# Output product of a two-layer decoder trunk: loads issued in strict order, residual halves and the next layer's loads behind them, late sums held, first splits behind evacuations

## The chip, the cores and the metric

The kernel runs on one core of one Trainium2 chip. The metric is the device time of one execution in microseconds; the time before is the median of three runs. The profiled execution is a further run, taken with the hardware profiler.

## The reference

Two post-norm layers on a sequence of 1024 tokens with width 1024. Layer 0 mixes tokens by differential attention with rotary keys, layer 1 by forgetting attention; each is followed by a gated MLP of width 2816 with a causal width-3 convolution on the gate branch. Cut to what matters here:

```python
def conv_ffn(x, w_in, conv_w, conv_b, w_out):
    gate, up = jnp.split(x @ w_in, 2, axis=-1)
    gate = lax.conv_general_dilated(gate, conv_w[:, None, :], ...) + conv_b
    return (jax.nn.silu(gate) * up) @ w_out

for i in range(DEPTH):                      # DEPTH = 2
    y = diff_attention(h, ...) if i == 0 else forgetting_attention(h, ...)
    h = layer_norm(alpha * h + y, ln1_g[i], ln1_b[i])
    f = conv_ffn(h, ffn_w_in[i], ffn_conv_w[i], ffn_conv_b[i], ffn_w_out[i])
    h = layer_norm(alpha * h + f, ln2_g[i], ln2_b[i])
```

The change lies in the last product, `@ w_out`, of both layers, and at the border to the stage before it.

## The kernel before

**Arithmetic.** All products are in split float32: an operand is copied by ScalarE into a rounded high part (L90) and VectorE subtracts it to get the low part (L92); three matmuls, high x high, high x low and low x high (L101 to L103), make one product of tiles. The function that does this is `split`, so a split is one instruction on ScalarE and one on VectorE.

**The MLP.** Both MLP products run as Strassen-like schemes: a 2 x 2 block product by seven block products m = 1 to 7 in place of eight. The up stage goes over 22 feature tiles f of 128 features; for each it makes the seven products in the order 1, 5, 6, 3, 7, 2, 4, four times 3 matmuls each. Some products accumulate in the PSUM bank of an earlier one (6, 7 and 4 on that of 1, 3 on that of 5), so the bank must have been read (evacuated) before: `take` does it, with a ScalarE copy (L1114) or a VectorE addition (L1116). When the last product of a tile is through, `gated` convolves, applies silu, multiplies, stores the gated tile to DRAM (`ad[f]`, L1156) and forms block sums of it in DRAM (`sd`): for f < 11 by plain stores, for f >= 11 by accumulating DMAs issued by GpSimd (POOL, L1163). The sums of the last two tiles, f = 20 and 21 (`last`), are kept as functions in `late_adds` and run at a step of the output product.

**The output product.** `down_steps` makes 64 steps in four passes over k = 0 to 10 (pairs of feature tiles): products (1, 2), (6, 5), (7, 3) and (4). A step is 4 x 3 matmuls for one product and one k; the last two k of a pass (the last eight of pass four) go as one group. Per k a pass loads strips of 128 x 512: `load_a` the activations (`ha`, L1210, from `ad` or `sd`), `load_b` the weights (`wb`, L1217, from `in_wd`); one weight block is loaded in pairs in other buffers (`wst` or `pt`). The strips lie in the 32 buffers that hold the operands of the up products 1, 5, 3 and 7 until these are through; later a strip is free when it has been split. `weights` makes differences of weight strips in place on VectorE (L1226, L1230). `make` splits both operands into one of six pairs of buffers. At the end of a product, `drain` (L1293) takes each bank into the accumulators `acc`; products 6, 7 and 4 (and 3) then go on in the bank just drained. The accumulators hold the residual, loaded from `hs` in halves by `half` (L1338).

**What sets the order.** The Python code traces the instructions in a step order: `when(i, ...)` puts loads, halves, norm and late sums at step i of the output product (step 0 is its first; negative steps lie in the up stage), and `Ffn.run` makes up to six operand pairs ahead. The framework then fixes at build time, with a model of its own of the durations, in which order each engine and each DMA queue takes its instructions; it may deviate from the traced order where data dependences allow it. At run time each queue is in that order, and semaphores hold an instruction until its operands and buffers are ready. All plain loads and stores are issued by SyncE (SP). `with self.tc.issue_after(ins)` ties the instructions in its block that run on the engine of `ins` behind `ins` in that engine's order, without a wait.

Of the kernel before, what the change touches and what calls it, by code (L numbers as in the profile page):

```python
# [3 lines left out]

# [10 lines left out]
ALU = mybir.AluOpType  # L15
# [30 lines left out]
PSF, PSN, PN17 = (0,), 3, 0  # L46
PN1, PN2, PN3 = 256, 0, 256
PF = (0, 0, 0, 0)
S2, S3 = 1, 0
M7, G4 = 15, 8  # L50
ORDER = (0, 2, 1, 3)
# [6 lines left out]
class Trunk:  # L58
# [1000 lines left out]
    def up_steps(self, l, acc):  # L1059

        nc = self.nc
        self.flip = False
        st, early = {}, []
        seq = [(0, 1), (1, 1), (0, 2), (1, 2), (2, 1), (2, 2)]
        seq += [(f, m) for m in (5, 6, 3, 7, 4) for f in (0, 1)]
        seq += [(2, 5), (2, 6), (2, 3), (2, 7), (3, 1), (2, 4)]
        seq += [(f, m) for f in range(3, NF) for m in (1, 5, 6, 3, 7, 2, 4) if (f, m) != (3, 1)]
        onto = {6: 1, 7: 1, 4: 1, 3: 5}

        def make(f, m):  # L1070
            d = st.setdefault(f, {})
            if m == 1:
                d["wg"] = self.tmp(pool=self.tt, tag="pt") if f == 2 else \
                    self.wp.tile([P, 1024], F32, tag="wst", name=self.nm("wg"), bufs=2)
                nc.sync.dma_start(d["wg"], self.i["wi"][l, f])
            elif m == 5:
                d["wu"] = self.tmp()
                nc.sync.dma_start(d["wu"], self.i["wi"][l, NF + f])
            d[m, "w"] = self.up_operand(d["wg"], d.get("wu"), m)


        def product(f, m):
            d = st[f]
            hl = d.pop((m, "w"))
            more = m in onto
            if more:
                d[m] = d[onto[m]]
            elif f < 3 and (m == 1 or (f, m) == (2, 2)):
                if f != 1 and m == 1:
                    early.append(self.sbank())  # L1090
                n = f == 1 or m == 2
                d[m] = early[-1][:, n * 512:n * 512 + 512]
            else:
                d[m] = self.mbank()
            for i in range(4):
                w = slice(i * P, i * P + P)
                self.mm3(d[m], hl[:, w], hl[:, 512 + i * P:512 + i * P + P], *self.x[m, i],
                         i == 0 and not more, i == 3, more)
                self.pulse()

        def take(f, m):


            d = st[f]
            ps = d[m]
            lo, hi = slice(0, 512), slice(512, 1024)
            if m == 1:
                d["g"] = self.qp.tile([P, 1024], F32, tag=f"q{1 - self.own}", name=self.nm("sg")) \
                    if f < 2 else self.tmp(pool=self.pp, tag="p")
            elif m == 5:  # L1110
                d["b"] = self.tmp(pool=self.tt, tag="pt")
            dst = d["b" if m in (5, 7, 4) else "g"][:, lo if m in (1, 2, 5, 7) else hi]
            if m in (1, 5, 6, 4):
                nc.scalar.copy(dst, ps)  # L1114
            else:
                nc.vector.tensor_tensor(dst, ps, dst, op=ALU.add)  # L1116

        def takes(f, m):
            if f == 2 and m in (1, 2):
                return  # L1120
            take(f, m)
            if (f, m) == (1, 4):
                take(2, 1)
            elif (f, m) == (2, 5):
                take(2, 2)
            if m == 4 and f > 1:
                self.gated(l, f, st.pop(f))
            elif f == 2 and m in (6, 3):
                self.gated(l, m == 3, st.pop(m == 3))

        return [([partial(make, *x)], partial(product, *x), partial(takes, *x)) for x in seq]
# [4 lines left out]
    def gated(self, l, f, d):  # L1136

        nc = self.nc
        cw, cb = self.cw[l], self.cb[l]
        g = d["g"]  # L1140
        t = self.tmp()
        nc.scalar.activation(t, g, AF.Identity, scale=cw[:, f, 2:3], bias=cb[:, f:f + 1])
        nc.vector.scalar_tensor_tensor(t[:, 1:], g[:, :1023], cw[:, f, 1:2], t[:, 1:],
                                       op0=ALU.mult, op1=ALU.add)
        nc.vector.scalar_tensor_tensor(t[:, 2:], g[:, :1022], cw[:, f, 0:1], t[:, 2:],
                                       op0=ALU.mult, op1=ALU.add)
        nc.scalar.activation(t, t, AF.Silu)
        if f == NF - 1:

            with self.tc.tile_critical():  # L1150
                nc.scalar.preload_act_table_set("natural_log_exp_and_others")
                nc.scalar.copy(t[:, :1], t[:, :1])
        k = f % (NF // 2)
        nc.vector.scalar_tensor_tensor(t[:, :512], t[:, :512], -1.0, d["b"][:, 512:], op0=ALU.mult, op1=ALU.mult)
        nc.vector.tensor_tensor(t[:, 512:], t[:, 512:], d["b"][:, :512], op=ALU.mult)
        nc.sync.dma_start(self.ad[f], t)  # L1156
        last = f > NF - 3
        e = (self.tmp() if last else g)[:, :512]
        nc.vector.tensor_tensor(e, t[:, :512], t[:, 512:], op=ALU.add)

        def adds():
            for out, x in ((self.ad[k][:, 512:], t[:, 512:]), (self.sd["6"][k], t[:, 512:]), (self.sd["3"][k], e)):
                nc.gpsimd.dma_start(out, x, accum_op=ALU.add)  # L1163

        if f == k:
            for r in ("6", "7", "3"):
                nc.sync.dma_start(self.sd[r][k], e)
        elif last:
            self.late_adds.append(adds)
        else:  # L1170
            adds()
# [9 lines left out]
    def down_steps(self, l):  # L1181
        nc = self.nc
        H = NF // 2
        a, b, acc = {}, {}, []
        self.norm2, self.late_adds = None, []
        outs = {1: (0, 0), 2: (0, 0), 6: (0, 1), 5: (1, 1), 7: (1, 1), 3: (0, 1), 4: (1, 0)}
        onto = {6: 1, 7: 1, 4: 1, 3: 5}
        passes = ((1, 2), (6, 5), (7, 3), (4,))
# [12 lines left out]
        def strip(name, dt=F32):  # L1201
# [2 lines left out]
            n_h += 1  # L1204
            return self.xp.tile([P, 512], dt, tag=("xl", "xh")[n_h % 2], name=self.nm(name))

        def load_a(m, k):

            a[m, k] = strip("ha")
            nc.sync.dma_start(a[m, k], self.sd[str(m)][k] if m in (3, 6, 7) else  # L1210
                              self.ad[k + (0 if m in (1, 5) else H)][:, lo if m < 3 else hi])

        def load_b(n, k):

            def load(t, r):
                b[r, k] = t
                nc.sync.dma_start(t, w[(r // 10 - 1) * H + k][:, lo if r % 10 == 1 else hi])  # L1217

            if n < 0 and k % 2 == 0:
                self.pair = self.wp.tile([P, 1024], F32, tag="wst", name=self.nm("wb"), bufs=2) if k % 4 else \  # L1220
                    self.tmp(pool=self.tt, tag="pt")
            for r in ((11,), (12, 22), (22, 12), (21,), (21,))[n]:
                load(self.pair[:, k % 2 * 512:k % 2 * 512 + 512] if n < 0 else strip("wb"), r)

        def sub(dst, x, y):
            nc.vector.tensor_tensor(dst, x, y, op=ALU.subtract)  # L1226
# [22 lines left out]
        def make(m, k):  # L1249
            nonlocal n_a  # L1250
            if m == 4 and k >= H - 3:
                at, bt = [[strip("oa", F32R) for _ in range(2)] for _ in range(2)]
            else:
                self.flip = not self.flip
                bt = self.wp.tile([P, 1024], F32R, tag="wh" if self.flip else "wl", name=self.nm("wo"))
                j = n_a % 6
                n_a += 1
                at = self.qtile(1 - self.own) if j == 0 else \
                    self.tp.tile([P, 1024], F32R, tag="of", name=self.nm("oa"), bufs=1) if j == 1 else \
                    self.pp.tile([P, 1024], F32R, tag="p", name=self.nm("oa"))  # L1260
                at, bt = [[t[:, lo], t[:, hi]] for t in (at, bt)]
            ops[m, k] = at, bt
            for t, src in zip((at, bt), (a.pop((m, k)), weights(m, k))):
                self.split(*t, src)

        banks = {}

# [67 lines left out]

        def half(tt, c):
            cs = slice(c * 512, c * 512 + 512)
            nc.sync.dma_start(acc[tt][:, cs], self.hs[tt][:, cs])  # L1338


        for tt in range(8):
            when(4, load_acc, tt)
            when(11 + tt if tt < 4 else 20 + tt, half, tt, int(tt > 3))
            when((30 if tt < 4 else 44) + tt, half, tt, int(tt < 4))

        def norm():
# [1 line left out]

        when(6, norm)
        for j in range(2):  # L1350
            when(9 + 3 * j, lambda j=j: self.late_adds[j]())
        m6 = len(steps) - (H + 1 - G4)
        when(m6 + S2, lambda: self.norm2.root(st[0]))
        for tt in range(4):
# [5 lines left out]
    def run(self):  # L1360
# [4 lines left out]
        self.resid = self.i["x"].rearrange("(t p) d -> t p d", p=P)  # L1365
        for l in range(2):
            self.own = (NP + l) % 2
            self.attention(l)
            self.ff.run()
            self.resid = self.hd  # L1370

# [246 lines left out]
```

## Time and profile before

| | |
|---|---|
| runs | 2447.15, 2448.49, 2451.36 us; median 2448.49 us |
| profiled execution | 2453.07 us, of it span 2451.3 us |
| mean granted clock of TensorE | 0.996 |
| TensorE busy | 2404.3 us of the span, 98% |
| VectorE, ScalarE, GpSimd busy | 1869.8, 1245.4, 198.8 us |
| moved by DMA | 312.20 MB, mean 127 GB/s |
| output product | from about 985 us to 1198 us in layer 0, from about 2225 us to the end in layer 1 |

In the listings, PE is TensorE, DVE VectorE, ACT ScalarE and POOL GpSimd; an engine's name with a q is its queue. A row of a list of waits has who waited, for whom, the total in us, how many times, and the longest. A row of a timeline has the start in us, the duration in us, engine, line, operation, output <- inputs by the program's names and, in square brackets, how long the engine stood idle before it and what ended that. A row of stretches has the stretch, its length, each engine's busy time with the number of its instructions in parentheses, then TensorE's granted clock as a share of full speed, the mean busy share of the 16 DMA engines and the GB/s that they moved.

### The profile page before, as it was taken

To read this page: it belongs to the slowest core of one execution; us is meant where nothing else is said; L and a number is where in the kernel's file an instruction comes from. 1 tells how busy PE (TensorE), PEld (TensorE's weight loads), DVE (VectorE), ACT (ScalarE), POOL (GpSimd) and SP (SyncE) were. 2 spreads that over 40 slices of the span, in tenths; PEclk is the share of its full clock that TensorE was granted. 3 is DMA by queue.
4 is the path that set the end of the run, shared out by engine and by line. 5 is a ranking of instruction groups with operands and counts; after the bars stand their busy time and mean duration, and the time that the engine had idled before them with its cause. 6 is when DMAs were issued, how large, how long until landed. Compare 5 with 4: busy or idle time off the path is not lost. (4 is left out here: it accounts for less than half of the span.)

```text
span 2451.3 us, 33031 instructions
## 1 busy us (share of the span) xinstructions
PE 2404.3 (98%) x11361; PEld 1982.9 (81%) x11361; DVE 1869.8 (76%) x3543; ACT 1245.4 (51%) x2342; POOL 198.8 (8%) x390
## 2 busy tenths in 40 slices
PE   9999999999999999999999999999999999999998
PEld 7888887777888887878778888888878888887787
DVE  5888888989777776667767777778898777776668
ACT  4656666556444444434445555555465444444344
POOL 2111111010000111000100000000010001110000
PEclk9999999999999999999999999999999999999999
DMA  6223324522433556965322222234223345559662
GB/s 184 66 78 96 93 78 122 169 86 78 168 116 133 130 125 172 308 196 175 110 74 67 67 68 67 67 101 141 92 91 133 121 141 123 118 129 308 216 203 84
DMA packets 140456, 312.20 MB, mean 127 GB/s; under 512 B 20816, under 2 KB 27984, under 8 KB 140288
## 3 DMA queue, kind: packets, MB, share of 16 engines
q1 hardware_dynamic: 129824, 291.67, 37.6%
q0 software_dynamic: 10176, 18.36, 4.6%
q8 instruction: 89, 1.46, 0.3%
q14 instruction: 79, 0.65, 0.1%
q10 hardware_dynamic: 288, 0.07, 0.0%
HBM read 194.21 MB, written 82.25 MB: 113 GB/s over the span
## 5 line engine op out<-in xcount | busy, mean ns | idle before, releaser
L101 PE MATMUL m<-xh,wh 128*128 128x512 f32 x768 | 314.2, 409 | 0.3 <-ACT xh L90 0.3
L102 PE MATMUL m<-xl,wh 128*128 128x512 f32 x768 | 301.7, 393 | 1.6 <-DVE xl L92 1.6
L103 PE MATMUL m<-xh,wl 128*128 128x512 f32 x768 | 303.1, 395 | 0.0
L101 PE MATMUL m<-xh,wo 128*128 128x512 f32 x656 | 255.5, 389 | 1.7 <-ACT pt L1114 1.7
L103 PE MATMUL m<-xh,wo 128*128 128x512 f32 x656 | 255.3, 389 | 0.0
L102 PE MATMUL m<-xl,wo 128*128 128x512 f32 x656 | 255.2, 389 | 0.0
L90 ACT ACTIVATE wo<-wg 128x512 fp32r<-128x512 f32 x168 | 106.0, 633 | 226.6 <-PE m L103 215.5
L543 DVE CUSTOM_DVE_ANT_0 s<-s,mask 128x384 f32<-128x384 f32 (+7 forms) x256 | 194.2, 759 | 31.9 <-PE s L537 30.9
L90 ACT ACTIVATE pt<-m 128x512 fp32r<-128x512 f32 (+3 forms) x285 | 131.3, 491 | 115.2 <-PE m L1401 111.2
L101 PE MATMUL m<-q,wo 128*128 128x512 f32 x472 | 184.8, 392 | 3.6 <-DVE pt L1116 3.6
L102 PE MATMUL m<-q,wo 128*128 128x512 f32 x472 | 184.3, 390 | 0.0
L103 PE MATMUL m<-q,wo 128*128 128x512 f32 x472 | 184.2, 390 | 0.0
L92 DVE TENSOR_TENSOR pt<-m,pt 128x512 fp32r<-128x512 f32 (+3 forms) x285 | 151.8, 557 | 39.7 <-ACT pt L90 37.9
L103 PEld LDWEIGHTS m<-xh,wl 128*128 128x128 f32 x768 | 144.7, 188 | 31.1
L101 PEld LDWEIGHTS m<-xh,wh 128*128 128x128 f32 x768 | 145.1, 189 | 26.7 <-DVE pt L92 1.9
L102 PEld LDWEIGHTS m<-xl,wh 128*128 128x128 f32 x768 | 145.3, 189 | 25.5 <-DVE xl L92 1.9
L528 POOL CAST qz<-q 64x128 fp32r<-64x128 f32 x256 | 97.9, 383 | 823.0 <-PE s L537 755.1
L90 ACT ACTIVATE wo<-t 128x512 fp32r<-128x512 f32 x132 | 82.7, 627 | 145.5 <-PE m L103 130.1
L101 PEld LDWEIGHTS m<-xh,wo 128*128 128x128 f32 x656 | 123.1, 188 | 27.9 <-ACT pt L1114 2.6
L103 PEld LDWEIGHTS m<-xh,wo 128*128 128x128 f32 x656 | 123.1, 188 | 26.0 <-DVE wo L92 0.4
L102 PEld LDWEIGHTS m<-xl,wo 128*128 128x128 f32 x656 | 123.2, 188 | 25.6
L536 PE MATMUL s<-q,q 128*128 128x512 f32 (+4 forms) x384 | 132.4, 347 | 2.1 <-ACT wst L581 1.3
(354 smaller groups left out, 5904.3 us busy)
## 6 DMA issues: line engine op xcount, KB each, us to landing
wb<-in_wd SPq DMA_DIRECT2D x142, 256.0 KB, 4.9
wst<-in_w SPq DMA_DIRECT2D x46, 512.0 KB, 3.7
t<-in_wi SPq DMA_DIRECT2D x44, 512.0 KB, 4.6
ad<-t SPq DMA_DIRECT2D x44, 512.0 KB, 3.2
ha<-ad SPq DMA_DIRECT2D x88, 256.0 KB, 7.8
wg<-in_wi SPq DMA_DIRECT2D x42, 512.0 KB, 3.6
ha<-sd SPq DMA_DIRECT2D x66, 256.0 KB, 2.8
q<-q SPq DMA_DIRECT2D x128, 128.0 KB, 2.2
```

The lines of the kernel that those rows point to most:

```text
L90: nc.scalar.activation(hi, src, AF.Copy, scale=1.0 if scale is None else scale)
L92: nc.vector.tensor_tensor(lo, src, hi.bitcast(F32), op=ALU.subtract)
L101: mm(out, wh, xh, start=start, stop=False)
L102: mm(out, wh, xl, start=False, stop=False)
L103: mm(out, wl, xh, start=False, stop=stop)
L528: nc.gpsimd.tensor_copy(qz[r:r + 64, :], q[r:r + 64, qt * P:qt * P + P])
L536: nc.tensor.matmul(sb[:, ks], q[:, qt * P:qt * P + P], kd[:, ks], start=True, stop=False)
L543: self.nc.vector.tensor_tensor_reduce(sb[:, :ln], sb[:, :ln], self.mask[:, 1024 - ln:], 1.0, BIG, ALU.add, ALU.min, mn)
```

## The change

- Loads of the output product (`load_a`, `load_b`) go through a new `load`, which ties each load on SP's queue behind the one traced before it (`self.ld` is the last).
- `half` is tied behind the last load traced; the second group of halves (four tiles, c = 1) moves from steps 24 to 27 to steps 35 to 38 (`R2` 31 for 20). `R1` is 11, as the number before.
- The whole SP traffic of layer 1's attention is tied behind layer 0's last load.
- The store of `ad[f]` for f = 20 and 21 is issued by POOL in place of SP.
- The three accumulating sums of each of these two tiles are placed at steps 14 and 18 in place of 9 and 12, and wait until the load traced last before them has landed.
- `take` records the last evacuation on ScalarE and on VectorE; in `make` the splits and the weight differences are tied behind them on their engines.

`EARLY_D` is defined and not used. No arithmetic is changed.

```diff
+EARLY_D, R1, R2, ADDS = 8, 11, 31, (14, 18)
...
-                nc.scalar.copy(dst, ps)
+                self.taken["a"] = nc.scalar.copy(dst, ps).ins
             else:
-                nc.vector.tensor_tensor(dst, ps, dst, op=ALU.add)
+                self.taken["v"] = nc.vector.tensor_tensor(dst, ps, dst, op=ALU.add).ins
...
-        nc.sync.dma_start(self.ad[f], t)
         last = f > NF - 3
+        (nc.gpsimd if last else nc.sync).dma_start(self.ad[f], t)
...
-                nc.gpsimd.dma_start(out, x, accum_op=ALU.add)
+                add = nc.gpsimd.dma_start(out, x, accum_op=ALU.add)
+                if last:
+                    self.tc.add_manual_dep(add.ins, self.ld.ins.name, mybir.DependencyInfo(
+                        mybir.DependencyClass.Sync, mybir.DependencyReason.DATA), reason="late sums")
...
+        def load(dst, src):
+            with self.tc.issue_after(self.ld.ins) if self.ld is not None else nullcontext():
+                self.ld = nc.sync.dma_start(dst, src)
+
         def load_a(m, k):
...
-            nc.sync.dma_start(a[m, k], self.sd[str(m)][k] if m in (3, 6, 7) else
-                              self.ad[k + (0 if m in (1, 5) else H)][:, lo if m < 3 else hi])
+            load(a[m, k], self.sd[str(m)][k] if m in (3, 6, 7) else
+                 self.ad[k + (0 if m in (1, 5) else H)][:, lo if m < 3 else hi])
...
-            for t, src in zip((at, bt), (a.pop((m, k)), weights(m, k))):
-                self.split(*t, src)
+            with self.tc.issue_after(self.taken["a"]), self.tc.issue_after(self.taken["v"]):
+                for t, src in zip((at, bt), (a.pop((m, k)), weights(m, k))):
+                    self.split(*t, src)
...
-            nc.sync.dma_start(acc[tt][:, cs], self.hs[tt][:, cs])
+            with self.tc.issue_after(self.ld.ins):
+                nc.sync.dma_start(acc[tt][:, cs], self.hs[tt][:, cs])
...
-            when(11 + tt if tt < 4 else 20 + tt, half, tt, int(tt > 3))
+            when(R1 + tt if tt < 4 else R2 + tt, half, tt, int(tt > 3))
...
-            when(9 + 3 * j, lambda j=j: self.late_adds[j]())
+            when(ADDS[j], lambda j=j: self.late_adds[j]())
...
-            self.attention(l)
+            with self.tc.issue_after(self.ld.ins) if l else nullcontext():
+                self.attention(l)
```

More of the change, by code (lines that the diff above doesn't have):

```diff
@@ L1 @@
 import math
-from contextlib import ExitStack
+from contextlib import ExitStack, nullcontext
 from functools import partial
@@ L1062, in up_steps @@
         self.flip = False
-        st, early = {}, []
+        st, early, self.taken = {}, [], {}
         seq = [(0, 1), (1, 1), (0, 2), (1, 2), (2, 1), (2, 2)]
@@ L1184, in down_steps @@
         a, b, acc = {}, {}, []
-        self.norm2, self.late_adds = None, []
+        self.norm2, self.late_adds, self.ld = None, [], None
         outs = {1: (0, 0), 2: (0, 0), 6: (0, 1), 5: (1, 1), 7: (1, 1), 3: (0, 1), 4: (1, 0)}
@@ L1205, in strip, with fetch @@
             return self.xp.tile([P, 512], dt, tag=("xl", "xh")[n_h % 2], name=self.nm(name))
+        def load(dst, src):
+            with self.tc.issue_after(self.ld.ins) if self.ld is not None else nullcontext():
+                self.ld = nc.sync.dma_start(dst, src)
         def load_a(m, k):
             a[m, k] = strip("ha")
-            nc.sync.dma_start(a[m, k], self.sd[str(m)][k] if m in (3, 6, 7) else
-                              self.ad[k + (0 if m in (1, 5) else H)][:, lo if m < 3 else hi])
+            load(a[m, k], self.sd[str(m)][k] if m in (3, 6, 7) else
+                 self.ad[k + (0 if m in (1, 5) else H)][:, lo if m < 3 else hi])
         def load_b(n, k):
-            def load(t, r):
+            def fetch(t, r):
                 b[r, k] = t
-                nc.sync.dma_start(t, w[(r // 10 - 1) * H + k][:, lo if r % 10 == 1 else hi])
+                load(t, w[(r // 10 - 1) * H + k][:, lo if r % 10 == 1 else hi])
             if n < 0 and k % 2 == 0:
@@ L1222, in load_b @@
             for r in ((11,), (12, 22), (22, 12), (21,), (21,))[n]:
-                load(self.pair[:, k % 2 * 512:k % 2 * 512 + 512] if n < 0 else strip("wb"), r)
+                fetch(self.pair[:, k % 2 * 512:k % 2 * 512 + 512] if n < 0 else strip("wb"), r)
         def sub(dst, x, y):
```

## The prediction

> **What bounds the kernel now.** First the page's busy times, then the list of waits of TensorE (PE), summed over the run.
>
> ```profile
> PE 2404.3 (98%) x11361; PEld 1982.9 (81%) x11361; DVE 1869.8 (76%) x3543; ACT 1245.4 (51%) x2342; POOL 198.8 (8%) x390
> ...
> PE s L101 <- DVE acc L1293: 9.2, 4, 3.4
> ...
> PE m L101 <- DVE pt L1116: 3.6, 2, 1.8
> PE m L101 <- ACT pt L1114: 1.7, 2, 1.3
> ```
>
> TensorE is busy for 98% of the span, so only its own gaps can be won. Three waits belong to the stretch that the diff touches: before the first matmul of an output product that reuses a PSUM bank it waits for the drain of that bank (L1293, 9.2 us in four waits), and at the end of the up products for an evacuation (L1116 and L1114, 5.3 us in four). The next view cuts both layers' stretches into slices of 5 us; after the times come TensorE's busy time and, at the end of a row, granted clock, DMA share and GB/s.
>
> ```profile
> 980.00:985.00 5.00, 4.31 (x13) 3.46 (x14) 4.25 (x7) 1.59 (x2) 0.00 (x0) 0.72 1.05 390
> 985.00:990.00 5.00, 5.00 (x22) 4.05 (x22) 3.22 (x5) 4.01 (x7) 0.00 (x0) 0.94 1.00 368
> ...
> 1050.00:1055.00 5.00, 4.20 (x12) 3.37 (x13) 4.93 (x12) 1.95 (x4) 0.00 (x0) 0.66 0.75 256
> ...
> 2220.00:2225.00 5.00, 3.17 (x15) 2.30 (x14) 3.09 (x5) 2.92 (x4) 0.00 (x0) 1.00 1.05 399
> 2225.00:2230.00 5.00, 5.00 (x24) 4.14 (x23) 4.36 (x5) 3.73 (x6) 0.00 (x0) 1.00 1.05 387
> 2230.00:2235.00 5.00, 5.00 (x24) 4.14 (x23) 2.00 (x4) 2.70 (x5) 0.00 (x0) 1.00 0.36 133
> 2235.00:2240.00 5.00, 5.00 (x24) 4.14 (x23) 4.30 (x7) 2.12 (x4) 2.68 (x3) 1.00 0.81 186
> 2240.00:2245.00 5.00, 5.00 (x24) 4.14 (x23) 0.00 (x0) 0.00 (x0) 0.00 (x0) 1.00 1.09 249
> ...
> 2290.00:2295.00 5.00, 3.18 (x8) 2.00 (x7) 5.00 (x12) 2.71 (x5) 0.00 (x0) 0.50 0.35 105
> 2295.00:2300.00 5.00, 5.00 (x21) 4.06 (x20) 5.00 (x10) 2.22 (x4) 0.00 (x0) 0.87 0.66 207
> ```
>
> The gaps cost more than their length: after three of the four places the granted clock falls. While busy, TensorE loses 4.31 x 0.28 + 5.00 x 0.06 = 1.5 us after the evacuation waits of layer 0, 4.20 x 0.34 = 1.4 us after the drain waits of layer 0, and 3.18 x 0.50 + 5.00 x 0.13 = 2.2 us after those of layer 1; at 2220 the clock stays at 1.00. So the evacuations are worth 5.3 + 1.5 = **6.8 us**, the drains 9.2 + 1.4 + 2.2 = **12.8 us**, together 19.6 us (0.8%). That is the most these edits can bring.
>
> Behind the waits stand in-order engines. The timelines of the last layer show it:
>
> ```profile
> 2209.27 0.69 DVE L92 TENSOR_TENSOR q<-ha,q 128x512 fp32r<-128x512 f32 x1
> ...
> 2220.56 0.63 ACT L90 ACTIVATE q<-ha 128x512 fp32r<-128x512 f32 x1 [2.85 <-DMA ha<-ad]
> 2221.22 0.69 DVE L92 TENSOR_TENSOR q<-ha,q 128x512 fp32r<-128x512 f32 x1 [2.11 <-ACT q L90]
> 2221.83 0.68 DVE L1116 TENSOR_TENSOR pt<-m,pt 128x512 f32<-128x512 f32 x1
> 2222.57 0.50 PE L101 MATMUL m<-q,wo 128*128 128x512 f32 x1 [1.82 <-DVE pt L1116]
> ...
> 2286.06 0.69 DVE L1226 TENSOR_TENSOR wb<-wb,wb 128x512 f32<-128x512 f32 x1 [6.80 <-DMA wb<-in_wd]
> ...
> 2287.40 1.28 DVE L1293 SCALAR_TENSOR_TENSOR acc<-acc,s 128x512 f32<-128x512 f32 x2
> 2288.82 0.47 PE L101 MATMUL s<-wo,oa 128*128 128x512 f32 x1 [3.40 <-DVE acc L1293]
> 2292.95 0.80 PE L101 MATMUL s<-wo,oa 128*128 128x512 f32 x1 [1.82 <-DVE acc L1293]
> ...
> 1043.92 0.69 DVE L1226 TENSOR_TENSOR wb<-wb,wb 128x512 f32<-128x512 f32 x1 [7.47 <-DMA wb<-in_wd]
> ```
>
> At 2222 a split of the output product (L92), placed ahead of the evacuation, waits for a load, and the evacuation waits behind it. At 2286 a weight difference for k = 5 of the second pass, needed ten steps (some 25 us) later, holds VectorE for 6.80 us while the drains of the first pass stand behind it. Layer 0 does the same (7.47 us).
>
> **The change, part by part.**
>
> *Splits behind evacuations.* No instruction is added; only order. In trace order one operand pair, (1, 0), precedes the evacuation of product 7 instead of about five. The evacuations then wait for TensorE alone: 6.8 us gone, and I take all of it; the bounds are 0 and 6.8. What is late next: the splits that stood ahead. On VectorE these are, from 2209.27 to 2221.22, ten of about 0.6 us, 6 us that move behind the evacuations. The cover is VectorE's idle time in 2220 to 2235 by the rows above, 1.91 + 0.64 + 3.00 = 5.6 us, and a step of 12 matmuls (24 in a slice of 5 us, so 2.5 us) asks for only two splits there. It is just enough on the whole, but the last gating shares the time, so I charge 1 us per layer, **2 us**; bounds 0 and the whole 6 us per layer.
>
> *Stores of f = 20 and 21 to POOL; late sums held.* SP's own waits, its queue, and POOL's:
>
> ```profile
> SPq L1156 <- ACTq L1150: 5.4, 1, 5.4
> ...
> 2227.32 0.96 SPq L1210 DMA_DIRECT2D ha<-ad  x2
> 2234.99 0.32 SPq L1156 DMA_DIRECT2D ad<-t  x1
> ...
> 2208.77 0.89 POOL L1163 DMA_DIRECT2D ad<-t  x1 [16.38 <-DVE wo L92]
> 2235.37 0.86 POOL L1163 DMA_DIRECT2D ad<-t  x1 [23.92 <-DVE t L1155]
> ...
> 994.91 1.16 POOL L637 MEMSET wf<- 128x128 f32 x1
> 1192.22 0.81 POOL L1537 TENSOR_TENSOR acc<-acc,lg 128x256 f32<-128x256 f32 x1 [196.15 <-ACT acc L1536]
> ```
>
> SP stood from 2228.3 to 2235.0 before the store of f = 21 and moved 133 GB/s instead of 387: 3.3 us of loads at full rate. On POOL the store holds nothing up at once, but load (2, 10) reads it, and in strict order all later loads stand behind that load; only the loads between gain, so I count 3 us of earlier arrival, none of it on TensorE by itself. POOL pays one more issue of about 0.9 us per store. The three sums of each of the two tiles (0.79 MB) move from 2208 and 2235 to behind the landing of a load of the second pass, k = 2 and k = 4. In 2235 to 2245 the loads and sums moved 2.18 MB where 387 GB/s would be 3.87 MB: 4.4 us of load time, estimated for one set and the restart. It is not removed but put 20 to 30 us later, beside the loads for k = 4 to 6. Behind the waiting sums POOL has only the memset of L637 and then nothing until 1192: free. Who reads the sums is load k = 9 and 10 of the second pass, ten steps (about 25 us) behind their issue: no wait. Without that cover all loads behind them would stand for a landing.
>
> *Loads strict, residual halves behind, R2 31 for 20.* The queue ahead of the load that held VectorE:
>
> ```profile
> 2269.34 0.84 SPq L1338 DMA_DIRECT2D acc<-hs  x2
> ...
> 2277.70 1.07 SPq L1338 DMA_DIRECT2D acc<-hs  x2
> 2278.87 0.62 SPq L1217 DMA_DIRECT2D wb<-in_wd  x1
> ...
> 2278.87 7.10 DMA wb<-in_wd
> ```
>
> These are the first and the last of four such pairs: eight residual halves of 256 KB, 2.1 MB or 5.4 us at 387 GB/s, go out ahead of this load though they belong to steps 24 and later. Behind the loads of steps 30 to 51 they no longer compete. With the 3 us above, the k = 5 weights land about 8 us earlier, more than the 6.80 and 7.47 us for which VectorE stood. So the long wait goes. But the second wait at each boundary (1.82 us here) comes from splits placed between the drains, and nothing in the diff orders a split or a weight difference against a drain. Of 12.8 us I take **9.7 us**, leaving about 1.5 us per layer; the bounds are 12.8 us and a loss, below. The moved halves are wanted at the drains of step 38 and later and can be issued some ten steps earlier: free.
>
> *Next layer's loads behind.* Its first slab is loaded early and used late:
>
> ```profile
> 1046.21 0.42 SPq L110 DMA_DIRECT2D wst<-in_w  x1
> 1150.80 0.33 SPq L1217 DMA_DIRECT2D wb<-in_wd  x1
> 1179.61 1.07 ACT L90 ACTIVATE wh<-wst 128x1024 fp32r<-128x1024 f32 x1 [0.45 <-PE s L103]
> ```
>
> From the last load at 1150.80 to the use there are 29 us, enough for loads of a few us: nothing lost. If it came later than that, the gate logits of layer 1 would wait.
>
> **Sum:** 6.8 + 9.7 - 2.0 = 14.5 us. The profiled execution took 2453.07 us, 4.6 us above the median of the runs, 2448.49; it becomes 2438.6, and the median **2434.0 us**.
>
> On the clock, the page "TensorE: Matmul & The Clock Gate" of the Trainium skill, Part 1, says that the half rate follows after an idle window of about 3.4 us. This trace differs: 0.66 and 0.72 follow waits of 2.5 and 1.8 us, while 1.00 follows another of 1.8 us. By the page only the wait of 3.40 us would lose clock, and the most to be won would be 2.9 us smaller than by the rows; the rows decide here.
>
> **The rivals.** (a) *Only the evacuations gain* (chance 0.18). Weight differences for k = 6 or 7 are placed ahead of the drains in place of k = 5, since strict order brings their loads forward, and VectorE stands as before. For: nothing ties them to the drains. Against: 8 us of earlier arrival. 6.8 - 2.0 = 4.8 us, 2443.7 us.
>
> (b) *No change* (0.12): as (a), and the moved splits starve the first steps by as much as the evacuations give, 3.4 us per layer, within the 6 us bound. 2448.5 us. Against it is VectorE's 5.6 us of idle time.
>
> (c) *Slower* (0.12): the held sums fall beside the very loads that VectorE waits for. A stand of 6.80 us gave TensorE 5.2 us of waits and 2.2 us of lost clock. The drains turn to a net loss when they cost 4.8 us more than now, that is 2.4 us per layer or a stand of about 9 us. With a set's whole 4.4 us on top of the 6.80, and as much again for k = 7, a stand of 15.6 us costs 8.8 us more per layer: 17.6 - 4.8 = 12.8 us slower, 2461.3 us. Against: loads then have lost 2.1 MB of halves from their queue. The page "DMA: Bandwidth & Descriptors" of the Trainium skill, Queues, rings and completion order, says that an engine takes packets in turn from the queues that have work, which speaks for this case; in the queues' shares over 2235 to 2245 (packets, MB, share of the DMA engines) the trace agrees:
>
> ```profile
> q1 hardware_dynamic: 638, 1.44, 50.7%
> q0 software_dynamic: 393, 0.74, 44.2%
> ```
>
> The sums' queue took nearly half of the engines for a third of the bytes.
>
> The forecast itself has 0.58. Its own range is 2428 to 2440: all 19.6 us won with the scatter of the runs below, and half of the drains above. The whole range reaches over (a) and (b), to 2450; below 2427 there is nothing to win. About 0.2% (4.9 us) is what a measurement of this kernel tells from no change; since (a) lies at that bound, half of its chance goes to each side: faster 0.67, same 0.21, slower 0.12.
>
> **What would show it.** Right: no wait of TensorE for L1116 or L1114 in the up products; VectorE's idle time before the first L1226 after the first pass under 3 us; DMA rate near 387 in the slice where SP now stands; no residual half between the loads of the first 25 steps; POOL's sums some 20 to 30 us later. Wrong: TensorE waiting for L92 in the first output steps, a longer wait for L1293, or loads standing behind the read of f = 21's store until splits run dry.

## The result, and the profile after

The changed kernel takes 2433.72 us, the median of five runs (2432.52 to 2439.96), where the kernel before takes 2448.49: ratio 0.994, interval 0.9925 to 0.9955, some 14.7 us less. A second series gave 0.9941 (0.9928 to 0.9954); each ratio in this document is taken against the kernel before in the same series. The forecast was 2434.0 us. The execution whose profile is read first is the slowest of its five (2439.96 us, span 2438.2); the second series has a profile of its own, of 2434.04 us, span 2432.3. Of the lines named here, the numbers are one to nine higher than before: evacuations are L1115 and L1117, the drain L1302, the weight differences L1234 and L1238, splits L91 and L93, matmuls L102 to L104, loads L1213.

The list of TensorE's waits after, first profile, the rows of the touched stretch:

```profile
PE s L102 <- DVE acc L1302: 4.0, 2, 2.3
...
PE s L104 <- DVE oa L93: 0.6, 1, 0.6
```

Of the waits at the end of the up products, 5.3 us before, no row is left in this stretch; the drain waits (TensorE waiting for a drain) fell from 9.2 to 4.0 us, all of it in layer 0. In the second profile of the same kernel no drain wait is left at all. The timelines show VectorE's stand, its idle time for the k = 5 weights before the first drain. First profile:

```profile
1038.12 0.69 DVE L1234 TENSOR_TENSOR wb<-wb,wb 128x512 f32<-128x512 f32 x1 [4.98 <-DMA wb<-in_wd]
...
1045.01 0.50 PE L102 MATMUL s<-wo,oa 128*128 128x512 f32 x1 [1.71 <-DVE acc L1302]
...
1100.29 0.69 DVE L1234 TENSOR_TENSOR wb<-wb,wb 128x512 f32<-128x512 f32 x1 [1.86 <-DMA wb<-in_wd]
...
1107.63 0.50 PE L102 MATMUL s<-wo,oa 128*128 128x512 f32 x1 [2.25 <-DVE acc L1302]
...
2272.36 0.69 DVE L1234 TENSOR_TENSOR wb<-wb,wb 128x512 f32<-128x512 f32 x1 [1.35 <-DMA wb<-in_wd]
```

Second profile:

```profile
959.84 1.25 ACT L1143 ACTIVATE t<-p,cb,cw 128x1024 f32<-128x1024 f32 x1
...
1033.96 0.69 DVE L1234 TENSOR_TENSOR wb<-wb,wb 128x512 f32<-128x512 f32 x1 [2.17 <-DMA wb<-in_wd]
...
1098.63 1.87 DVE L1302 SCALAR_TENSOR_TENSOR acc<-acc,m 128x512 f32<-128x512 f32 x3
...
2266.95 0.69 DVE L1234 TENSOR_TENSOR wb<-wb,wb 128x512 f32<-128x512 f32 x1 [2.38 <-DMA wb<-in_wd]
```

The stand was 7.47 and 6.80 us before; it is 4.98 and 1.35 us in the one execution and 2.17 and 2.38 in the other. After the stand of 4.98 us TensorE still waits at the end of pass one, 1.71 us (at 1045.01); after the stands of 1.35 to 2.38 us of this kernel it does not. The other 2.25 us of the 4.0 lie at another place, the end of pass two (1107.63), where TensorE waited for nothing before: there a weight difference of a later pass, at 1100.29, stands ahead of the drains in its turn. At the place that the change was made for, 9.2 us became 1.7.

To compare executions without the scatter of the rest of the kernel, two clocks are used below, both started by the first activation of feature tile f = 20 (L1142 before, L1143 after; 959.84 in the listing above). The *k = 5 clock* is the start of the weight difference that stands right before the first drain of pass one: 1033.96 - 959.84 = 74.1 us. The *pass-two clock* is the start of the group of three drains near the end of pass two: 1098.63 - 959.84 = 138.8 us. Before, in layer 0, they are 1043.92 - 959.01 = 84.9 us (the row of the weight difference is shown in the prediction) and 150.0 us from these rows:

```profile
959.01 1.25 ACT L1142 ACTIVATE t<-p,cb,cw 128x1024 f32<-128x1024 f32 x1
...
1109.00 1.88 DVE L1293 SCALAR_TENSOR_TENSOR acc<-acc,m 128x512 f32<-128x512 f32 x3
```

The table has both clocks (layer 0 / layer 1), worked out from the same rows of each trace, TensorE's waits for evacuations and for drains (us in the touched stretch of both layers, at the ends of all passes), and the measured ratio to the kernel before. A step of 0.001 is 2.4 us. The experiments it names follow.

| kernel | k = 5 clock | evacuations | drains | pass-two clock | ratio (interval) |
|---|---|---|---|---|---|
| before | 84.9 / 84.3 | 5.3 | 9.2 | 150.0 / 149.1 | 1 |
| after, first profile | 77.0 / 73.3 | 0 | 4.0 | 144.0 / 138.3 | 0.994 (0.9925 to 0.9955) |
| after, second series | 74.1 / 74.3 | 0 | 0 | 138.8 / 139.0 | 0.9941 (0.9928 to 0.9954) |
| splits only | 84.8 / 82.2 | 0 | 13.8 | 149.8 / 147.0 | 1.0003 (0.9994 to 1.0012) |
| stores and sums only | 84.5 / 81.4 | 0 | 9.8 | 150.0 / 146.2 | 1.0004 (0.9995 to 1.0013) |
| halves only | 80.7 / 78.6 | 4.4 | 3.0 | 145.6 / 142.1 | 0.9971 (0.996 to 0.9983) |
| order only | 79.2 / 74.7 | 5.5 | 0 | 143.6 / 141.1 | 0.9969 (0.9958 to 0.998) |
| order and splits | 79.4 / 74.4 | 0 | 3.8 | 144.4 / 139.5 | 0.9967 (0.9956 to 0.9979) |
| all but splits | 75.3 / 73.3 | 0.4 | 0.6 | 140.6 / 139.0 | 0.9928 (0.9914 to 0.9941) |
| all but halves | 74.1 / 74.7 | 0 | 1.5 | 141.4 / 138.7 | 0.9952 (0.994 to 0.9965) |
| all but held sums | 75.7 / 75.8 | 0 | 4.7 | 143.6 / 141.3 | 0.9952 (0.9939 to 0.9964) |

Each clock and each wait is one execution; the ratio is the measurement. In the first profile 2.3 us of the drain waits lie at the end of pass two, in "all but held sums" 2.2 us, and in "all but splits" and "all but halves" all of them; in the other rows all lie at the end of pass one.

In the rows without a wait for evacuations to speak of, the k = 5 clock orders the drain waits at the end of pass one. Per layer they are nothing up to 75.3 us, 1.1 to 1.7 us at 75.7 to 77.0, 3.8 us at 79.4, and 4.5 to 8.0 us from 81.4 on. The length of the stand does not: in "order and splits", layer 0, it is 2.29 us, with 3.8 us of drain waits. One row needs care: in layer 0 of "stores and sums only" the clock is no landing of weights (experiment 8).

### The profile page after: what moved, and what is told of

Read it like the earlier page. It is cut to its first block, busy times and chain, and to the rows that moved or that the text cites. A ratio compares the mean times of both kernels' runs of the same rounds, so it can differ in the third digit from the quotient of the medians.

```text
span 2438.2 us, 32989 instructions
## 1 busy us (share of the span) xinstructions
PE 2399.7 (98%) x11361; PEld 1981.7 (81%) x11361; DVE 1866.9 (77%) x3543; ACT 1244.7 (51%) x2342; POOL 200.2 (8%) x394
## 5 line engine op out<-in xcount | busy, mean ns | idle before, releaser
L102 PE MATMUL m<-xh,wh 128*128 128x512 f32 x768 | 314.6, 410 | 1.3 <-ACT xh L91 1.3
L104 PE MATMUL m<-xh,wl 128*128 128x512 f32 x768 | 303.4, 395 | 0.0
L104 PE MATMUL m<-xh,wo 128*128 128x512 f32 x656 | 255.3, 389 | 0.0
L102 PE MATMUL m<-xh,wo 128*128 128x512 f32 x656 | 255.2, 389 | 0.0
L91 ACT ACTIVATE wo<-wg 128x512 fp32r<-128x512 f32 x168 | 106.0, 632 | 226.0 <-PE m L104 215.2
L91 ACT ACTIVATE pt<-m 128x512 fp32r<-128x512 f32 (+3 forms) x285 | 131.3, 491 | 115.2 <-PE m L1412 111.3
L102 PE MATMUL m<-q,wo 128*128 128x512 f32 x472 | 184.1, 390 | 0.0
L104 PE MATMUL m<-q,wo 128*128 128x512 f32 x472 | 183.7, 389 | 0.0
L93 DVE TENSOR_TENSOR pt<-m,pt 128x512 fp32r<-128x512 f32 (+3 forms) x285 | 151.9, 557 | 39.7 <-ACT pt L91 38.1
L104 PEld LDWEIGHTS m<-xh,wl 128*128 128x128 f32 x768 | 145.0, 189 | 31.1
L102 PEld LDWEIGHTS m<-xh,wh 128*128 128x128 f32 x768 | 145.4, 189 | 27.6 <-DVE pt L93 2.1
L103 PEld LDWEIGHTS m<-xl,wh 128*128 128x128 f32 x768 | 145.6, 190 | 25.4 <-DVE xl L93 1.8
L91 ACT ACTIVATE wo<-t 128x512 fp32r<-128x512 f32 x132 | 82.7, 626 | 146.0 <-PE m L104 130.0
L104 PEld LDWEIGHTS m<-xh,wo 128*128 128x128 f32 x656 | 123.2, 188 | 25.8 <-DVE wo L93 0.4
L102 PEld LDWEIGHTS m<-xh,wo 128*128 128x128 f32 x656 | 123.2, 188 | 25.6
```

What stands on the lines that cost most here:

```text
L91: nc.scalar.activation(hi, src, AF.Copy, scale=1.0 if scale is None else scale)
L93: nc.vector.tensor_tensor(lo, src, hi.bitcast(F32), op=ALU.subtract)
L102: mm(out, wh, xh, start=start, stop=False)
L103: mm(out, wh, xl, start=False, stop=False)
L104: mm(out, wl, xh, start=False, stop=stop)
```

## The experiments

**1. The splits alone** (label e1_splits_only), on the kernel before:

```diff
+            with self.tc.issue_after(self.taken["a"]), self.tc.issue_after(self.taken["v"]):
                 for t, src in zip((at, bt), (a.pop((m, k)), weights(m, k))):
                     self.split(*t, src)
```

> The kernel before with one edit: the splits of the output product are placed behind the last evacuations; loads, stores, halves and sums stay as before. Theory (parts add up): the waits of TensorE for the two evacuations (5.3 us) and the lost clock behind them (1.5 us) go, the drain waits stay near 9.2 us: 2448.5 - 6.8 = 2441.7 us. With the 2.0 us that I charged for late splits it would be 2443.7, with waits of TensorE for L93 in the first output steps. Rival (the loads do it all): the evacuations wait as before for something else that stands on VectorE or ScalarE, 2448 us.

Measured: 1.0003 (0.9994 to 1.0012), no gain. The waits and the timeline say where the 5.3 us went:

```profile
PE s L101 <- DVE acc L1294: 13.8, 4, 6.7
...
1043.40 0.69 DVE L1226 TENSOR_TENSOR wb<-wb,wb 128x512 f32<-128x512 f32 x1 [7.63 <-DMA wb<-in_wd]
1046.16 0.77 PE L101 MATMUL s<-wo,oa 128*128 128x512 f32 x1 [6.72 <-DVE acc L1294]
```

No evacuation is waited for any more, and the drains are waited for 13.8 us, where it was 9.2. TensorE comes earlier to the end of pass one and meets the same late weights: the k = 5 clock in layer 0 is 84.8 us for 84.9. The upstream wait had covered part of the downstream one. In layer 1 both clocks are 2.1 us lower than in the profile before; the interval leaves room for a gain of 1.5 us at most, so that part of this is the scatter of single executions. Both theories were wrong, the sum of parts and the rival that let the evacuations wait as before.

**2. All but the splits** (e2_all_but_splits): the changed kernel with the lines above taken back.

> The changed kernel without the order of splits behind evacuations. Theory (parts add up): the evacuation waits come back, 5.3 us and 1.5 us of clock, the drains stay near 4 us: 2433.7 + 6.8 = 2440.5 us. Rival: with the loads in strict order the operand for which the split stood (it waited 2.85 us) lands earlier, so the evacuations hardly wait either, 2434 to 2436 us.

Measured: 0.9928 (0.9914 to 0.9941), the rival's time or better. In its list of waits only this is left of the two places:

```profile
PE s L102 <- DVE acc L1301: 0.6, 1, 0.6
...
PE m L102 <- ACT p L1115: 0.4, 1, 0.4
```

So the evacuations run free without the edit that was made for them, and the whole gain is there. The interval overlaps that of the changed kernel (0.9941, 0.9928 to 0.9954), so taking the edit out is not shown to be faster; that it is needed is refuted.

**3. All but the halves** (e3_halves_free): the halves not tied, and

```diff
-EARLY_D, R1, R2, ADDS = 8, 11, 31, (14, 18)
+EARLY_D, R1, R2, ADDS = 8, 11, 20, (14, 18)
```

> The changed kernel with the residual halves neither tied behind the loads nor moved (R2 20 for 31). Theory (it is the 2.1 MB of halves ahead of the k = 5 weights that made VectorE stand): the stand before the drains grows by about 5.4 us in each layer, drain waits go from 4.0 us back to about 9, 2433.7 + 8.8 = 2442.5 us. Rival (the order of the loads and the store on POOL are enough): stand under 5 us, 2434 to 2436 us.

Measured: 0.9952 (0.994 to 0.9965). The median, 2437.46 us, lies between the two expectations, and the ratio is not separated from the changed kernel. The stand did not come back:

```profile
1036.49 0.69 DVE L1234 TENSOR_TENSOR wb<-wb,wb 128x512 f32<-128x512 f32 x1 [2.18 <-DMA wb<-in_wd]
```

With the loads in strict order the halves no longer delay the k = 5 weights (74.1 and 74.7 us). SyncE's timeline shows where they fit in, in this kernel and then in the second profile of the changed one:

```profile
1019.25 0.91 SPq L1213 DMA_DIRECT2D wb<-in_wd  x2
1020.20 3.04 SPq L1347 DMA_DIRECT2D acc<-hs  x6
1029.92 0.32 SPq L1213 DMA_DIRECT2D ha<-sd  x1
```

```profile
1015.63 0.88 SPq L1213 DMA_DIRECT2D wb<-in_wd  x2
1026.47 0.33 SPq L1213 DMA_DIRECT2D ha<-sd  x1
```

Before the loads for k = 5 SyncE itself stands, in the changed kernel 9.9 us for a split (L93), which is what frees a strip to load into. Six halves go out in this gap; the stand for the split is then 4.8 us.

**4. All but the held sums** (e4_sums_free): the dependence of the sums on a load taken out, `ADDS` (9, 12) for (14, 18).

> The changed kernel with the late sums not held behind loads and called at steps 9 and 12, as before. Theory (a set of sums costs the loads 4.4 us wherever it stands ahead of the k = 5 weights, and one of the two sets stands there in both kernels): the sums are back near 2208 and 2235, the stand before the drains changes by less than 2 us, 2432 to 2436 us. Rival 1 (the held sums beside the k = 5 loads are what leaves 4 us of drain waits in layer 0): these go, 2430 us. Rival 2 (holding them is what frees the loads): the stand grows by 4.4 us per layer, half of it on TensorE with its clock, 2439 us.

Measured: 0.9952 (0.9939 to 0.9964), median 2437.36 us, drain waits 4.7 us. The k = 5 clock is 75.7 and 75.8 us, 1.6 and 1.5 us later than in the second profile of the changed kernel, but between the 77.0 and 73.3 us of the first. That is the first expectation for the weights; the time is 1.4 us above its range. Rival 1 is refuted, since the drain waits did not go; rival 2 asked for a delay of 4.4 us, more than either comparison shows. The ratio is not separated from the changed kernel's, so what holding the sums is worth stays open.

**5. The changed kernel again** (c0_after), no edit.

> The changed kernel once more, as the measure for the other runs of this chip: 2433.7 us, ratio to the kernel before 0.994; drain waits of TensorE near 4 us and no wait for an evacuation of the up products.

Measured: 2434.87 us, 0.9941; its rows stand in the section on the result. The drain waits were expected near 4 us and were none: with one kernel they differ by that much from one execution to the next.

**6. The halves alone** (s1_halves_only), on the kernel before: each half tied behind the last load, R2 31.

> The kernel before with one part alone: the residual halves stand behind the load that was issued last, and the second set of four begins at step 31 for 20. Splits, loads, stores, sums and the next layer as before. Theory A (each part has its own wait): the k = 5 weights land 5.4 us earlier, the drain waits fall from 9.2 to about 2 us with their clock, the evacuation waits stay at 5.3: 2448.5 - 9 = 2439.5 us. Theory B (one late supply; taking the halves back in the changed kernel cost about 3 us only): 3 to 4 us, 2445 us, with several us of drain waits left.

Measured: 0.9971 (0.996 to 0.9983), 7.1 us; between the theories. The weights start 4.2 and 5.7 us earlier, close to the 5.4 us of the halves' bytes, and the drain waits fall by 6.2 us; the evacuation waits stay:

```profile
PE m L102 <- DVE pt L1117: 3.2, 2, 1.6
PE s L102 <- DVE acc L1297: 3.0, 2, 2.0
...
PE m L102 <- ACT pt L1115: 1.2, 1, 1.2
```

**7. The order alone** (s2_order_only), on the kernel before: `load` ties each load behind the one before, nothing else.

> The kernel before with one part alone: every load of the output product is issued behind the one before it. Splits, halves, stores, sums and the next layer as before. Theory A (each part has its own wait): order by itself removes nothing from the queue, so the waits stay, 2446 to 2449 us. Theory B (the operands for the splits that stand ahead of the evacuations, and the k = 5 weights, come late because later loads are issued ahead of them): the evacuation waits go and half of the drain waits, 2437 to 2441 us.

Measured: 0.9969 (0.9958 to 0.998), 7.6 us. Neither theory had it whole: the drains are free altogether, and the evacuations wait as before.

```profile
PE m L102 <- DVE pt L1117: 5.5, 2, 3.3
```

SyncE's timeline shows why. In the prediction's rows the k = 5 weights are issued at 2278.87, the last of several loads and halves, and take 7.10 us to land. With the loads in order they go at 2267.48, although ten halves stand ahead of them in one block, and 3.2 us later the difference has them:

```profile
2257.13 5.87 SPq L1343 DMA_DIRECT2D acc<-hs  x10
...
2267.48 0.81 SPq L1210 DMA_DIRECT2D wb<-in_wd  x2
...
2270.72 0.69 DVE L1231 TENSOR_TENSOR wb<-wb,wb 128x512 f32<-128x512 f32 x1 [0.22 <-DMA wb<-in_wd]
```

From the start of the layer's clock (2201.78 before, 2196.04 here) the issue is at 77.1 and 71.4 us: 5.7 of the 9.6 us by which the weights come earlier in this layer are an earlier issue, the rest a quicker landing.

**8. Stores and sums alone** (s3_stores_and_sums), on the kernel before: the two stores on POOL, the sums held.

> The kernel before with one part alone: the stores of the last two gate tiles on POOL, and their sums held behind loads of the second pass. Splits, loads, halves and the next layer as before. Theory A (each part has its own wait): 3 us of earlier arrival only, 2445 to 2449 us. Theory B (4.4 us of sums and 3 us of standing taken away ahead of the k = 5 weights is what freed the boundary): 7 us earlier landing, drain waits under 3 us, 2440 us.

Measured: 1.0004 (0.9995 to 1.0013), theory A by its time. But the trace repeats experiment 1 by other means: no wait for L1115 or L1117 in the stretch, and

```profile
PE s L102 <- DVE acc L1300: 9.8, 4, 3.5
```

The split that held the evacuation in the prediction's rows stood 2.85 us for its load and started 18.8 us after the start of the layer's clock; here it stands 1.62 us and starts at 14.8 us. So with the first sums and the store out of the way the first strips land sooner. The gain is waited away at the drains. In layer 0, though, VectorE does not stand there for the k = 5 weights but for the split of `wf`, the gate weights of the next layer, and the weight difference then follows without a wait:

```profile
1041.96 0.29 DVE L93 TENSOR_TENSOR wf<-t,wf 128x128 fp32r<-128x128 f32 x1 [6.45 <-ACT wf L91]
```

Stores and sums or the order of splits, each alone, free the evacuations. This fits experiment 2, which needs no order of splits.

**9. Drains first** (d1_drains_first), on the kernel before, no DMA edit:

```diff
+            with self.tc.issue_after(self.drained) if m not in (1, 2) and k > 3 else nullcontext():
                 for t, src in zip((at, bt), (a.pop((m, k)), weights(m, k))):
                     self.split(*t, src)
```

> The kernel before, loads, stores, halves and sums untouched; the weight differences and splits for k = 4 and later of the second to fourth pass are placed behind the last drain of the pass before (VectorE's and ScalarE's order alone). Theory V (the late weights of k = 5 cost time only because the drains stand behind the difference that waits for them; TensorE needs them some 25 us later): the drain waits go from 9.2 us to under 2, the evacuation waits stay near 5, about as with the loads in order alone, 2443 us. Theory S (the loads as such are too late): TensorE waits for the operands of k = 5 in place of the drains, no gain, 2448 us or more.

**10. Drains first, and the splits** (d2_drains_first_splits): that and the edit of experiment 1.

> As the run above, and the first splits of the output product placed behind the evacuations: two changes of order on VectorE and ScalarE, and none of loads, stores, halves or sums. Theory V: both places are free, nothing of the 19.6 us is left to wait for, 2430 to 2435 us, as fast as the changed kernel. Theory S: the time that is won at the evacuations comes back as waits of TensorE for operands of the second pass, as it came back at the drains in the splits alone, 2445 us or more.

Measured: 1.0004 (0.9994 to 1.0013) and 0.9992 (0.9982 to 1.0001), the times of theory S. The waits of the first kernel are those of theory V: 1.6 us for drains and 4.7 us for evacuations. The edit had a side effect, so these times do not decide. It also ties the operands for k = 4 and later of pass four, which TensorE needs at once. In the second kernel, layer 1:

```profile
PE s L102 <- DVE wo L92: 4.3, 1, 4.3
...
2410.00:2415.00 5.00, 5.00 (x24) 4.14 (x23) 5.00 (x11) 1.80 (x7) 0.00 (x0) 1.00 0.00 0
2415.00:2420.00 5.00, 1.66 (x8) 1.04 (x6) 5.00 (x5) 0.49 (x1) 0.00 (x0) 0.93 0.49 200
```

The pass-two clock ends before that place. It is 143.4 and 142.6 us with the first edit alone, for 150.0 and 149.1 before. With both edits it is 144.5 and 138.7 us (layer 0, layer 1), where the splits alone had 149.8 and 147.0 and the changed kernel without a drain wait 138.8 and 139.0:

```profile
959.29 1.25 ACT L1142 ACTIVATE t<-p,cb,cw 128x1024 f32<-128x1024 f32 x1
...
1040.05 0.29 DVE L92 TENSOR_TENSOR wf<-t,wf 128x128 fp32r<-128x128 f32 x1 [2.15 <-ACT wf L90]
...
1103.83 1.88 DVE L1295 SCALAR_TENSOR_TENSOR acc<-acc,m 128x512 f32<-128x512 f32 x3
...
2201.62 1.25 ACT L1142 ACTIVATE t<-p,cb,cw 128x1024 f32<-128x1024 f32 x1
...
2340.34 1.87 DVE L1295 SCALAR_TENSOR_TENSOR acc<-acc,m 128x512 f32<-128x512 f32 x3
```

Up to there theory V holds whole in layer 1, with no load moved, and for half of the gain in layer 0, where TensorE still waited 2.5 us for a drain and 1.6 us for a split. The row at 1040.05 shows what stood ahead of the first drain there: again the split of `wf`, which the new tie leaves out and which layer 1 does not have. One execution of each kernel carries this; a version that ties only passes two and three was not run.

**11. Order and splits** (s5_order_and_splits), on the kernel before, nothing else.

> The kernel before with two parts: the loads in order and the first splits behind the evacuations; halves, stores, sums and the next layer as before. If the two places are worth about 7 us each once the other one is free, and the splits free the one and the order the other: 2434 to 2437 us, all that the changed kernel gains. If the halves and sums ahead of the k = 5 weights still hold the drains once TensorE comes 5 us earlier: 4 to 5 us of drain waits, 2440 us.

Measured: 0.9967 (0.9956 to 0.9979), the second case. The splits add nothing to the order (0.9969) even here: 5.5 us of evacuation waits go and 3.8 us of drain waits come, since the weights are no earlier than with the order alone (79.4 for 79.2 in layer 0). All of the 3.8 us lie in layer 0; in layer 1 the weights are at 74.4 us, as early as in the changed kernel, and both places are free. Only in layer 0 do loads of the next layer go out ahead of the k = 5 weights, and VectorE stands for the first of them:

```profile
PE s L102 <- DVE acc L1299: 3.8, 2, 2.5
...
1029.23 0.33 SPq L636 DMA_DIRECT2D t<-in_wf  x1
...
1034.47 0.29 DVE L93 TENSOR_TENSOR wf<-t,wf 128x128 fp32r<-128x128 f32 x1 [2.92 <-ACT wf L91]
```

In the changed kernel this load goes out at 1142 us or later. So the tie of the next layer's loads may be a part that the gain needs; it was not tried by itself.

**12. All but the splits, drains first** (d3_best).

> The changed kernel without the order of splits behind the evacuations, and with the weight differences and splits for k = 4 and later behind the last drain of the pass before. Theory V: no drain wait in any execution (the changed kernel had 4.0 us in one profile and none in the other) and hardly an evacuation wait: 2430 to 2432 us, and less scatter above. If differences placed behind the drains starve the first steps of the second pass: new waits for L93, 2434 us or more.

Measured: 0.997 (0.9959 to 0.9982), slower than without the new tie. No drain wait is left, as theory V had it, and the pass-two clock is 139.4 and 138.3 us, no worse than the best. The new waits do not stand in the first steps of the second pass but in pass four, the side effect of experiment 9, in both layers:

```profile
1170.00:1175.00 5.00, 4.18 (x21) 2.89 (x19) 5.00 (x8) 0.63 (x1) 0.00 (x0) 1.00 0.26 103
1175.00:1180.00 5.00, 3.66 (x16) 2.23 (x17) 5.00 (x8) 2.24 (x4) 0.00 (x0) 1.00 0.80 320
...
2405.00:2410.00 5.00, 2.91 (x13) 2.06 (x11) 5.00 (x8) 0.63 (x1) 0.00 (x0) 1.00 0.24 97
2410.00:2415.00 5.00, 2.76 (x6) 1.72 (x7) 5.00 (x8) 2.17 (x4) 0.00 (x0) 0.54 0.80 322
2415.00:2420.00 5.00, 5.00 (x18) 3.68 (x16) 3.25 (x6) 0.76 (x2) 0.00 (x0) 0.78 0.00 0
```

TensorE idles 0.82 + 1.34 us in layer 0 and 2.09 + 2.24 us in layer 1, and loses 2.76 x 0.46 + 5.00 x 0.22 = 2.4 us of clock: 8.9 us. The lowest time measured is that of the changed kernel without its order of splits, 2431.52 us in the median (2430.78 to 2435.25).

## Why the prediction was right, and where it was not

**The two places were right, the split into parts was not.** The waits of 14.5 us and their clock were there to be won, and the second profile has none of them left. But the sum was built from two places that were taken as independent, 6.8 us for the splits and 9.7 us for the loads. They lie in series behind one late supply. What a place gives depends on the other: freeing the evacuations gains no time that was measured while the drains stand behind late loads (experiments 1, 8, 11). With all parts of the change the weights are at 73 to 77 us, and both places are free or nearly so, with the splits' edit or without it.

**That the time was hit within 0.3 us, 2433.72 for 2434.0, is in part luck.** In the second profile nothing is left of what the prediction priced at 19.6 us, not at 14.5, and the two profiled executions differ by 19.0 us (2453.07 and 2434.04). The charge of 2.0 us and the 3.1 us of drains that were to stay did not come. Against these 5.1 us stands another error: the forecast took off 4.6 us more because the profiled execution before lay that far above its median, and the second profile does not lie above its own (2434.87). The two nearly cancel. How much a median execution of the kernel before waits at these places is not known, since only one has a profile.

**Splits behind evacuations, 6.8 us, "I take all of it": the step that failed.** Alone it gives nothing (1.0003), and without it the gain is whole (0.9928). The working asked what was late next only among the splits, not at the next wait of TensorE, though the row of 6.80 us stood in it.

**The 2.0 us for late splits: mis-sized.** In neither profile does TensorE wait for L93 in the first output steps (the row of 0.6 us above lies in pass four), so the charge is 0.

**Strict order: left out of the sum.** The working gave it no term of its own and let the 8 us of earlier weights come from halves (5.4) and stores (3). Order alone brought the weights 5.7 us (layer 0) and 9.6 us (layer 1) forward and gave 7.6 us. The halves alone gave 4.2 and 5.7 us, as sized, and 7.1 us of time. Once the order is there, the halves cost no delay of the weights, since they go out while SyncE stands for a strip (experiment 3). The two overlap; adding their 7.6 and 7.1 us up to 14.7, the whole gain, would be chance: the evacuation waits remain in each.

**Stores to POOL.** That the DMA rate would be near 387 GB/s where SyncE stood was wrong. The store no longer stands in its queue, and the read of the stored tile does, 6.7 us for 6.7 before:

```profile
SPq L1213 <- DMA ad<-t: 6.7, 1, 6.7
...
2228.86 7.47 SPq L1213 DMA_DIRECT2D ha<-ad  x2
...
2230.00:2235.00 5.00, 5.00 (x24) 4.14 (x23) 3.70 (x7) 4.74 (x9) 0.55 (x1) 1.00 0.42 163
2235.00:2240.00 5.00, 5.00 (x24) 4.14 (x23) 3.62 (x7) 1.95 (x4) 0.00 (x0) 1.00 0.55 176
```

The sentence that all later loads stand behind that load was right; the forecast of the rate did not follow from it.

**Held sums.** They were costed as put later, not removed, and no gain was counted for them. Experiment 4 does not contradict this: without holding them the weights are at 75.7 and 75.8 us, within the 73.3 to 77.0 of the changed kernel. Rival (c), a stand grown by the sums, did not occur: 4.98 us at the most for 7.47.

**Drains, 9.7 of 12.8 us.** The 1.5 us per layer left over was put down to splits between the drains. Instead the rest is uneven from run to run: 4.0 us of waits in layer 0 of one profile, 1.7 us of it at the end of pass one, nothing in layer 1 and nothing in the other. The 2.3 us at the end of pass two were in no term. The stand was to be under 3 us; it was so in three of four layers, but by the table the clock and not the stand is the sign.

**Halves and next layer.** Four halves (R1) still go among the first loads; "no residual half between the loads of first 25 steps" was too much, since only the second group moves. The next layer's first split still waits for TensorE alone, 0.45 us as before, so nothing was lost by the tie, as forecast:

```profile
1175.60 1.06 ACT L91 ACTIVATE wh<-wst 128x1024 fp32r<-128x1024 f32 x1 [0.45 <-PE s L104]
```

What the working left out is what the tie keeps away. In the kernel before, the load of `wf` goes out behind the k = 5 weights, so nothing showed; in experiments 7, 8, 9 and 11, which have no such tie, it comes ahead of them or of the drains, and VectorE stands 2.2 to 6.5 us for it.

**Rivals (a) and (b)** did not occur. Without the order of the loads and the halves something like them does: experiments 1 and 8 have the time of case (b), through another mechanism, since what took the gain was not a starved split but the drain wait that had been there.

## What to carry over

Waits of the same engine that lie behind one late supply do not add up: before pricing a wait, ask when the next resource on the path arrives if the engine comes there earlier. Measure the supply's arrival from a fixed event upstream (here 84.9 against 74.1 us); an edit that leaves it unchanged only moves the wait. The other way is to take the waiting instruction out of the way of what stands behind it (experiment 9). In a shared load queue, putting loads in the order of their use was worth as much as taking 2.1 MB out of it (0.9969 and 0.9971).

## What the runs showed of the hardware

The granted clock does not follow from the length of a wait alone. After TensorE's wait of 6.72 us in the first experiment it was 0.50 and 0.59:

```profile
1045.00:1050.00 5.00, 2.90 (x6) 1.82 (x6) 5.00 (x11) 2.53 (x6) 0.00 (x0) 0.50 0.78 208
1050.00:1055.00 5.00, 4.71 (x13) 3.80 (x14) 4.33 (x10) 1.53 (x3) 0.00 (x0) 0.59 0.64 235
```

In the order alone a wait of 3.31 us is followed by 0.66. In the changed kernel it stays at 1.00 after the wait of 2.25 us at 1107.63:

```profile
980.93 0.80 PE L102 MATMUL m<-q,wo 128*128 128x512 f32 x1 [3.31 <-DVE pt L1117]
...
980.00:985.00 5.00, 4.07 (x12) 3.25 (x13) 4.25 (x7) 1.83 (x3) 0.00 (x0) 0.66 1.05 393
```

```profile
1110.00:1115.00 5.00, 5.00 (x23) 4.13 (x23) 2.91 (x5) 1.65 (x3) 0.00 (x0) 1.00 0.82 293
```

Before the change a wait of 1.79 us, at 980.69, was followed by 0.72, and one of 1.82 us, at 2222.57, by 1.00 (the slices are in the prediction). The Trainium skill, "TensorE: Matmul & The Clock Gate", Part 1, puts the fall behind an idle window of about 3.4 us; by that rule the waits of 1.8 us would have cost no clock, and here one did and another did not. What else sets it was not found.
